# The last chunk's forward and backward scans interleaved, with the long convolution dealt out between their steps

## The chip, the cores and the metric

One core of one Trainium2 chip runs the whole kernel in one launch. The metric is the device time of an execution in microseconds (us); lower is better. The core has five engines with a queue of instructions each: TensorE (PE, matrix products and transposes), VectorE (DVE), ScalarE (ACT), GpSimd (POOL) and SyncE (SP), which here only issues DMA transfers. Each engine works its queue strictly in order and waits on semaphores for the others. Matrix products write to PSUM, of which this kernel uses eight banks of 128 x 512 f32; everything else lives in SBUF or in device memory.

## What is computed

One layer of a generator over 2048 tokens of width 1024, with 256 context tokens ahead. One projection feeds three mixers, whose outputs are concatenated, projected, scaled and added to the input; a layer norm and a gated MLP with a 3x3 depthwise convolution follow.

```python
def _mixer(h, lp, h0_f, h0_b):
    proj = h @ lp['w_in']
    a_val, a_gate, _, _, _, u_pool = jnp.split(proj, IN_SPLITS, axis=-1)
    ya = _conformer_conv(a_val, a_gate, lp)
    yb, st_f, st_b = _ssd_branch(proj, lp, h0_f, h0_b)
    yc = _pool_mixer(u_pool, lp)
    return jnp.concatenate([ya, yb, yc], axis=-1) @ lp['w_out'], st_f, st_b

def _conformer_conv(a_val, a_gate, lp):          # 256 channels, 31 taps, 15 tokens to either side
    u = a_val * jax.nn.sigmoid(a_gate)
    u = _dwconv1d(u, lp['conv_dw_w'], lp['conv_dw_b'], (CONV_K // 2, CONV_K // 2))
    u = jax.nn.silu(_layer_norm(u, lp['conv_ln_g'], lp['conv_ln_b']))
    return u @ lp['conv_pw_w'] + lp['conv_pw_b']

def _gated_rms_norm(y, z, gain):                 # y = forward scan + backward scan
    v = y.astype(F32) * jax.nn.silu(z.astype(F32))
    v = v * lax.rsqrt(jnp.mean(v * v, axis=-1, keepdims=True) + RMS_EPS)
    return (v * gain.astype(F32)).astype(z.dtype)
```

The SSD branch is a linear recurrence over tokens (8 heads of 64, state of 128, a 4-tap convolution ahead), run once forward and once backward. A scan is cut into sub-chunks: within one, a masked product of tokens with tokens; between them, a state of 128 x 512 is handed on. The forward scan goes up the tokens, the backward scan down, so the backward scan of the last sub-chunk needs no other one.

## The kernel before

Tokens are worked in four chunks of 512, a scan in sub-chunks of 128 (four a chunk; `f3_2` is the forward scan of chunk 3, sub-chunk 2, `b3_2` the backward one). All large products are f32 split into a high and a low part, three matrix products for one (`mm3`, lines L114 to L116; a weight is loaded at L108 and split at L101 and L102).

*Sweep one* takes the chunks upwards (`chunk`). For each it projects the input, applies the 4-tap convolutions of both directions on DVE (L266; forward result `uf` stays in SBUF, backward result `ub` is stored to `scr_ub`), runs the forward scan (its result `y_f` is stored to `scr_yf`, L508), the pool branch (`ps2`, `ps4`, `pr`, `pl`), the 31-tap convolution, and the gate projection z (`zproj`): four products (`zt`, L552), transposed on PE (`zT`, L557), SiLU on ACT (`zs`, L559), stored to `scr_zs` (L560). For chunk 3 z comes last in the code.

The 31-tap convolution (`conv_branch`) is 30 multiply-adds on DVE for each of two halves of 128 channels, 512 tokens each (`c31p`, in a PSUM bank; the bias and tap 0 by ACT, L589). Its result lags by 15 tokens, so chunk 3 has a tail of 15 more columns (`c31t`): 60 multiply-adds of 128x15, at the same line L592. `conv_post` follows: transposes `ct`, copy `ctv`, statistics `cst`, normalization `ctv` (L625), transposes back `cb`, SiLU (L630), product `pw` (L634), result `ya` stored to `scr_yac` (L637). The pool branch stores to `scr_yac` too.

*Sweep two* takes the chunks downwards. `bwd` reloads `ub` as eight tiles of 128x512 (`ubr`, L719, on ACT's queue) and runs the backward scan. `rest` gates each sub-chunk: forward result `yfr` (L732) and `zsr` (L734) are loaded by SP, added and multiplied on DVE (L736, L737), squared on ACT, `rstd` (`rv`, `rr`, `rq`, `yrs`; L121 to L128), scaled (L742), transposed on PE (`yt`, L745) and split (`ybh`, `ybl`). Then `yac` reloads the conv and pool outputs (L702), `mix` projects everything (`o`; its first operand is the conv output), adds it to the input (L782, L783), and the MLP follows after the last chunk. The code of `bwd` for chunk 2 stands ahead of the mix of chunk 3.

A scan step is `ssd_in`, then `ssd_out`. `ssd_in`: load the row of cumulated decays `E` (L353), eight Relu and one Exp on ACT (L355, L356), transposes and token products `bps` on PE, copy `btm` on ACT, mask `gtm` (L367) and `E` times `gtm` on DVE (L369), transposes `xps`, two products `xde`, `xdt` on DVE. `ssd_out`: state product `st` and state update (L406), `yo`, `y` (L414), `yd`, `y` (L419). The banks are few: one for `bps` and `xps` (pool `si`), two for `st`, `yo`, `yd` (`so`), one for all transposes of convolution, pool, z and gate (`lo`), four for the products (`mm`).

What order the instructions take on each engine is set when the program is built: a scheduler takes the code, estimates times, and puts the instructions of all engines in a fixed order, within the dependences and the number of buffers of each tile. It does not follow the order of the code where something else is ready.

## Time and profile before

| what | value |
|---|---|
| runs, us | 2604.77, 2612.76, 2610.20 (median 2610.2) |
| the profiled execution, us | 2605.01 |
| its span, us | 2603.3 |
| its mean granted PE clock | 0.957 |
| PE, DVE, ACT, POOL busy, share of the span | 92%, 69%, 44%, 50% |

The span runs from the first to the last instruction. A granted clock of 1 is full speed of TensorE. The profile gives the time by line and operation, the idle time of each engine with what ended it ("DVE x <- ACT y" is idle time of DVE in front of x, which y released), and the chain of work that ended last. The stretch in which sweep one ends and sweep two starts lies at about 553 to 871 us of the span. Below, `DVE`, `PE` and so on stand ahead of a line number; a name ends in `_f` or `_b` by the direction of the scan.

### The profile page before, as it was taken

Reading aid. Unit: us, or ns where it says so; the run is one execution under the profiler, and the core shown is the slowest. Engines: PE = TensorE matmul, PEld = TensorE weight load, DVE = VectorE, ACT = ScalarE, POOL = GpSimd, SP = SyncE. Lnnn points to the kernel's source line nnn. Section 1 sums busy time; section 2 is a strip of 40 time slices with the busy share of each in tenths; the row PEclk is TensorE's granted clock in tenths of the full one; section 3 lists DMA queues with packets and bytes.
Section 4 is the critical chain, followed back from the end, with each engine's and each line's share of the span. In section 5 each row is a group of like instructions: output and inputs, shape, how many; then the busy total and the mean of one; then the engine's idle time right before and its main releaser. Section 6 shows DMA issues by size and latency. Waiting matters only on the chain.

```text
span 2603.3 us, 31634 instructions
## 1 busy us (share of the span) xinstructions
PE 2403.8 (92%) x11338; PEld 1987.1 (76%) x11338; DVE 1791.9 (69%) x2681; ACT 1149.7 (44%) x1765; POOL 1303.9 (50%) x928
## 2 busy tenths in 40 slices
PE   6998999998768978899999999999999999899996
PEld 3776877776647767789998878888878888788885
DVE  5767968698948586576556596665696664876645
ACT  2657566747354334343334333344333344233342
...
GB/s 277 255 141 145 129 139 111 138 108 119 135 112 200 206 186 193 175 210 90 90 90 134 97 146 100 97 124 105 122 128 99 97 117 96 151 97 106 97 98 73
DMA packets 125838, 347.01 MB, mean 133 GB/s; under 512 B 19680, under 2 KB 24176, under 8 KB 125680
## 3 DMA queue, kind: packets, MB, share of 16 engines
...
## 4 chain that ended last, share of the span: by engine, by line
PE 61%; DVE 20%; DMA 6%; ACT 6%; issue 3%; POOL 2%; SPq 0%; ACTq 0%; DVEq 0%; POOLq 0%
PE d L114 6%; PE d L116 6%; PE d L115 6%; PE ug L114 5%; PE ug L115 5%; PE ug L116 5%; PE uv L114 5%; PE uv L115 5%; PE uv L116 5%; DVE c31p L592 2%; DVE fa L886 1%; DVE xt L783 1%; ACT E_f L355 1%; DMA x_c<-in_xT 1%; PE o L114 1%
## 5 line engine op out<-in xcount | busy, mean ns | idle before, releaser
L886 DVE SCALAR_TENSOR_TENSOR fa<-gbuf,cols,fa 128x512 f32<-128x512 f32 x704 | 523.6, 753 | 225.0 <-ACT fa L882 202.7
L916 DVE TENSOR_TENSOR gl<-g,gh 128x512 fp32r<-128x512 f32 x176 | 195.6, 1122 | 218.3 <-ACT gh L915 196.9
L102 POOL TENSOR_TENSOR wl_d<-wr_d,wh_d 128x1024 fp32r<-128x1024 f32 x88 | 222.1, 2524 | 210.7 <-ACT wh_d L101 210.7
L114 PE MATMUL ug<-h2h,wh_ug 128*128 128x512 f32 (+3 forms) x880 | 309.9, 352 | 18.1 <-DVE g L894 10.7
L102 POOL TENSOR_TENSOR wl_uv<-wr_uv,wh_uv 128x1024 fp32r<-128x1024 f32 x88 | 220.3, 2504 | 207.9 <-ACT wh_uv L101 207.9
L102 POOL TENSOR_TENSOR wl_ug<-wr_ug,wh_ug 128x1024 fp32r<-128x1024 f32 x88 | 214.5, 2437 | 192.1 <-ACT wh_ug L101 192.1
L115 PE MATMUL ug<-h2l,wh_ug 128*128 128x512 f32 (+3 forms) x880 | 309.0, 351 | 0.0
L116 PE MATMUL ug<-h2h,wl_ug 128*128 128x512 f32 (+3 forms) x880 | 308.7, 351 | 0.0
L114 PE MATMUL uv<-h2h,wh_uv 128*128 128x512 f32 x704 | 275.3, 391 | 9.0 <-DVE g L894 8.8
L115 PE MATMUL uv<-h2l,wh_uv 128*128 128x512 f32 x704 | 274.9, 390 | 0.0
L116 PE MATMUL uv<-h2h,wl_uv 128*128 128x512 f32 x704 | 274.6, 390 | 0.0
L115 PE MATMUL d<-wl_d,gh 128*128 128x512 f32 x704 | 273.9, 389 | 0.0
L114 PE MATMUL d<-wh_d,gh 128*128 128x512 f32 x704 | 273.8, 389 | 0.0
L116 PE MATMUL d<-wh_d,gl 128*128 128x512 f32 x704 | 263.8, 389 | 0.0
L915 ACT ACTIVATE gh<-g 128x512 fp32r<-128x512 f32 x176 | 110.9, 630 | 247.5 <-PE d L115 225.8
L114 PEld LDWEIGHTS ug<-h2h,wh_ug 128*128 128x128 f32 x880 | 168.8, 192 | 38.5 <-DVE g L894 11.9
L101 ACT ACTIVATE wh_ug<-wr_ug 128x1024 fp32r<-128x1024 f32 x88 | 93.2, 1059 | 221.4 <-PE uv L115 189.1
L115 PEld LDWEIGHTS ug<-h2l,wh_ug 128*128 128x128 f32 x880 | 168.8, 192 | 17.7
L116 PEld LDWEIGHTS ug<-h2h,wl_ug 128*128 128x128 f32 x880 | 168.6, 192 | 16.8
L592 DVE SCALAR_TENSOR_TENSOR c31p<-gl,cols,c31p 128x512 f32<-128x512 f32 x232 | 162.2, 746 | 20.3 <-ACT c31p L589 20.0
L114 PEld LDWEIGHTS uv<-h2h,wh_uv 128*128 128x128 f32 x704 | 132.6, 188 | 36.5 <-DVE g L894 9.6
L101 ACT ACTIVATE wh_uv<-wr_uv 128x1024 fp32r<-128x1024 f32 x88 | 93.2, 1059 | 144.7 <-PE ug L115 95.6
(391 smaller groups left out, 5485.6 us busy)
## 6 DMA issues: line engine op xcount, KB each, us to landing
wr_ug<-in_w_up SPq DMA_DIRECT2D x88, 512.0 KB, 3.6
wr_uv<-in_w_up SPq DMA_DIRECT2D x88, 512.0 KB, 3.5
wr_d<-in_w_dn SPq DMA_DIRECT2D x88, 512.0 KB, 3.6
wm<-in_w_mod SPq DMA_DIRECT2D x64, 256.0 KB, 3.8
wr_x<-in_w_x SPq DMA_DIRECT2D x32, 512.0 KB, 3.7
wr_o<-in_w_o SPq DMA_DIRECT2D x32, 512.0 KB, 4.1
wm<-in_w_mod SPq DMA_DIRECT2D x16, 512.0 KB, 8.0
x_c<-in_xT SPq DMA_DIRECT2D x32, 256.0 KB, 3.8
```

What stands on the lines that cost most here:

```text
L101: nc.scalar.activation(hi, src, AF.Copy)
L102: nc.gpsimd.tensor_tensor(lo, src, hi.bitcast(F32), AL.subtract)
L114: nc.tensor.matmul(out, a[0], b[0], start=first, stop=False)
L115: nc.tensor.matmul(out, a[0], b[1], start=False, stop=False)
L116: nc.tensor.matmul(out, a[1], b[0], start=False, stop=last)
L355: nc.scalar.activation(E[:, h, :], E[:, h, :], AF.Relu, bias=cum[:, d, s, h : h + 1], scale=-1.0)
L592: nc.vector.scalar_tensor_tensor(to[:, :m], gl[:, j, o + k : o + k + m], w[k], acc[:, :m], AL.mult, AL.add)
L783: nc.vector.scalar_tensor_tensor(xs[i][:, hsl], xs[i][:, hsl], ALPHA, m, AL.mult, AL.add)
L886: nc.vector.scalar_tensor_tensor(acc, G[:, dr : dr + 8, dc : dc + GW], wc[i], acc, AL.mult, AL.add)
L915: nc.scalar.activation(gh, gt[k], AF.Copy)
L916: nc.vector.tensor_tensor(gl, gt[k], gh.bitcast(F32), AL.subtract)
```

## The change

Chunk 3's forward and backward scan are put into one function, `turn`, which takes the place of the end of `chunk(3)` and of `bwd(3)`. It writes the steps in the order f0, f1, b3, b2, f2, b1, f3, b0, each with the start of the next one ahead of it.

- The backward inputs come in 128-token pieces (`ubs`, four loads of 512 KB on ACT's queue, two buffers) in place of the eight `ubr`.
- In the backward steps, `E` is in two tiles of 128x512, and `E`, `xde`, `xdt` and `xD` lie in buffers of the projection's input (`hhi`, `hlo`) that are no longer in use.
- A sub-chunk is gated when the later of its two directions is done: forward 0, 1 and backward 3, 2 are stored to `scr_yf` and read back by the gate; forward 2, 3 and backward 1, 0 are not stored.
- z is split in `zpart` and `zturn`; its projections stand in the code between the first forward steps and its transposes after the start of backward step 3. The pool branch stands between the two halves of the z projections.
- The 15-column tail becomes, for each channel half, one product of 128x465 (15 columns by 31 taps, the input read through overlapping windows, `slide`) and one sum over the taps (`tensor_reduce`); its `conv_post` comes first.
- The main convolution is a generator that hands back after every ten taps and is resumed between the steps, first half of the channels, then the second; its `conv_post` runs when it is used up, between the gates of sub-chunks 1 and 3.

Cut to its core, the diff:

```diff
+def slide(v, m, taps):
+    return bass.AP(tensor=v.tensor, offset=v.offset, ap=[list(v.ap[0]), [1, m], [1, taps]])
...
+        def buf(tag, alt):
+            if spare:
+                return self.p1.tile([P, 512], F32R, tag=alt, name=f"{tag}_{name}", bufs=8).bitcast(F32)
+            return sp.tile([P, 512], F32, tag=tag, name=f"{tag}_{name}", bufs=SB)
+
         r = {}
         if want_y:
-            E = sp.tile([P, 8, P], F32, tag="E", name=f"E_{name}", bufs=SB)
-            nc.sync.dma_start(E, self.s[f"arow{key}"][d, s].unsqueeze(0).to_broadcast([P, 8, P]))
+            if spare:
+                E = [buf(f"E{g}", "hhi").rearrange("p (h l) -> p h l", h=4) for g in range(2)]
+            else:
+                E = [sp.tile([P, 8, P], F32, tag="E", name=f"E_{name}", bufs=SB)]
+            m = 8 // len(E)
+            Eh = [E[h // m][:, h % m, :] for h in range(8)]
+            for i, e in enumerate(E):
+                nc.sync.dma_start(e, self.s[f"arow{key}"][d, s, i * m : (i + 1) * m].unsqueeze(0).to_broadcast([P, m, P]))
...
-            E4 = E.rearrange("p (g h) l -> p g h l", g=2)
-            nc.vector.tensor_tensor(E4, E4, gtm.unsqueeze(2).to_broadcast([P, 2, 4, P]), AL.mult)
-            r["E"] = E
+            n = 2 // len(E)
+            for i, e in enumerate(E):
+                E4 = e.rearrange("p (g h) l -> p g h l", g=n)
+                nc.vector.tensor_tensor(E4, E4, gtm[:, i * n : (i + 1) * n, :].unsqueeze(2).to_broadcast([P, n, 4, P]), AL.mult)
+            r["E"] = Eh
...
-        xde = sp.tile([P, 512], F32, tag="xde", name=f"xde_{name}", bufs=SB)
+        xde = buf("xde", "hlo")
...
+        if last:
+            return hs, fwd, out
         self.ppool(c, hs)
         for s in range(SB - 1):
             fwd(s)
-        if not last:
-            self.zproj(c, hs)
+        self.zproj(c, hs)
         for s in range(NSUB):
             out(s)
             if s + SB - 1 < NSUB:
                 fwd(s + SB - 1)
         self.pool_branch(c)
-        self.conv_branch(c)
-        if last:
-            self.zproj(c, hs)
+        for _ in self.conv_branch(c):
+            pass
+
+    def turn(self, hs, fwd, out):
+        c = NCH - 1
+        nc, sp, pa = self.nc, self.sp, self.pa
+        cat = [None] * 8
+        ybh = pa.tile([P, 4, 512], F32R, tag="ybh", name=f"ybh{c}", bufs=1)
+        ybl = pa.tile([P, 4, 512], F32R, tag="ybl", name=f"ybl{c}", bufs=1)
+        ub, ins = {}, {}
+
+        def load(s):
+            b = pa.tile([P, 8, P], F32, tag="ubs", name=f"ubs{c}_{s}", bufs=2)
+            t0 = c * CH + s * P
+            nc.scalar.dma_start(b, self.s["ub"][:, :, t0 : t0 + P].rearrange("j p t -> p j t"))
+            ub[s] = [b[:, j, :] for j in range(8)]
+
+        def first(s):
+            ins[s] = self.ssd_in(1, c, s, ub[s], 0, True, f"b{c}_{s}", spare=True)
+
+        def scan(s):
+            return self.ssd_out(1, c, s, ins[s], f"b{c}_{s}")
+
+        rows = self.s[f"yf{c}"]
+        conv = self.conv_branch(c)
+        load(3)
+        load(2)
+        self.ppool(c, hs)
+        fwd(0)
+        next(conv, None)
+        zt = self.zpart(c, hs, 0, 2)
+        self.pool_branch(c)
+        out(0)
+        fwd(1)
+        next(conv, None)
+        zt = zt + self.zpart(c, hs, 2, 4)
+        first(3)
+        self.zturn(c, zt)
+        next(conv, None)
+        first(2)
+        y = scan(3)
+        nc.sync.dma_start(rows[3 * P : 4 * P, :], y)
+        load(1)
+        next(conv, None)
+        out(1)
+        fwd(2)
+        next(conv, None)
+        y = scan(2)
+        nc.sync.dma_start(rows[2 * P : 3 * P, :], y)
+        load(0)
+        first(1)
+        next(conv, None)
+        y = out(2, False)
+        fwd(3)
+        self.gate(c, 2, y, ybh, ybl)
+        next(conv, None)
+        y = scan(1)
+        first(0)
+        self.gate(c, 1, y, ybh, ybl)
+        for _ in conv:
+            pass
+        y = out(3, False)
+        self.gate(c, 3, y, ybh, ybl)
+        y = scan(0)
+        self.gate(c, 0, y, ybh, ybl)
+        for i in range(4):
+            cat[2 + i] = (ybh[:, i, :], ybl[:, i, :])
+        return cat
 
...
         n = self.width(c)
-        accs, tails = [], []
+        wv = self.cols[:, COFF["dw_w"] : COFF["dw_w"] + 2 * TAPS].rearrange("p (j k) -> p j k", k=TAPS)
+        if n > CH:
+            m = n - CH
+            tail = self.lp.tile([P, 2, 16], F32, tag="c31t", name=f"c31t_{c}", bufs=1)
+            for j in range(2):
+                prod = self.lp.tile([P, CH], F32, tag="c31", name=f"c31q_{c}_{j}", bufs=4)[:, 0 : m * TAPS].rearrange("p (t k) -> p t k", k=TAPS)
+                g = gl[:, j, CH : CH + m + TAPS - 1]
+                nc.vector.tensor_tensor(prod, slide(g, m, TAPS), wv[:, j, :].unsqueeze(1).to_broadcast([P, m, TAPS]), AL.mult)
+                nc.vector.tensor_reduce(tail[:, j, 0:m], prod, mybir.AxisListType.X, AL.add)
+                nc.scalar.activation(tail[:, j, 0:m], tail[:, j, 0:m], AF.Identity, bias=self.col("dw_b", j))
+            self.conv_post(c, [tail[:, j, 0:m] for j in range(2)], m, CH)
+        accs = []
         for j in range(2):
-            w = [self.col("dw_w", j * TAPS + k) for k in range(TAPS)]
             out = self.lp.tile([P, CH], F32, tag="c31", name=f"c31_{c}_{j}", bufs=4)
-            parts = [(out, self.bank(self.mm, f"c31p_{c}_{j}"), 0, CH)]
-            if n > CH:
-                tail = self.lp.tile([P, 16], F32, tag="c31t", name=f"c31t_{c}_{j}")
-                parts.append((tail, tail, CH, n - CH))
-                tails.append(tail[:, 0 : n - CH])
-            for dst, acc, o, m in parts:
-                nc.scalar.activation(acc[:, :m], gl[:, j, o : o + m], AF.Identity, bias=self.col("dw_b", j), scale=w[0])
-                for k in range(1, TAPS):
-                    to = dst if k == TAPS - 1 else acc
-                    nc.vector.scalar_tensor_tensor(to[:, :m], gl[:, j, o + k : o + k + m], w[k], acc[:, :m], AL.mult, AL.add)
+            acc = self.bank(self.mm, f"c31p_{c}_{j}")
+            nc.scalar.activation(acc, gl[:, j, 0:CH], AF.Identity, bias=self.col("dw_b", j), scale=wv[:, j, 0:1])
+            for k in range(1, TAPS):
+                nc.vector.scalar_tensor_tensor(out if k == TAPS - 1 else acc, gl[:, j, k : k + CH], wv[:, j, k : k + 1], acc, AL.mult, AL.add)
+                if k % 10 == 0:
+                    yield
             accs.append(out)
         self.conv_post(c, accs, CH, 0)
-        if n > CH:
-            self.conv_post(c, tails, n - CH, CH)
 
...
+            self.gate(c, s, self.ssd_out(1, c, s, ins[s], f"b{c}_{s}"), ybh, ybl)
```

The order of the built programs at the places that matter. Names carry the chunk, the sub-chunk and a running number. First DVE, where chunk 2's convolution has ended and chunk 3's 4-tap convolutions (`ca_f`, `ca_b`, `ub`, `uf`) run; before:

```order
L592 SCALAR_TENSOR_TENSOR c31t_3_1_5935<-gl3_5002,cols_105,c31t_3_1_5935 128x15
L266 SCALAR_TENSOR_TENSOR ca_b3_2_5483<-raw3_2_5471,cols_105,ca_b3_2_5483 128x515
L266 SCALAR_TENSOR_TENSOR uf3_2_5475<-raw3_2_5471,cols_105,ca_f3_2_5476 128x512
L592 SCALAR_TENSOR_TENSOR c31t_3_1_5935<-gl3_5002,cols_105,c31t_3_1_5935 128x15
L266 SCALAR_TENSOR_TENSOR ub3_2_5482<-raw3_2_5471,cols_105,ca_b3_2_5483 128x515
L592 SCALAR_TENSOR_TENSOR c31t_3_1_5935<-gl3_5002,cols_105,c31t_3_1_5935 128x15 x2
L592 SCALAR_TENSOR_TENSOR c31p_3_0_5869<-gl3_5002,cols_105,c31p_3_0_5869 128x512 x4
```

After, the tail stands right behind the last tap of chunk 2 (`c31_2_1`):

```order
L691 SCALAR_TENSOR_TENSOR c31_2_0_4739<-gl2_3724,cols_105,c31p_2_0_4740 128x512
L691 SCALAR_TENSOR_TENSOR c31_2_1_4772<-gl2_3724,cols_105,c31p_2_1_4773 128x512
L681 TENSOR_TENSOR c31q_3_0_5650<-gl3_5002,cols_105 128x465
L681 TENSOR_TENSOR c31q_3_1_5654<-gl3_5002,cols_105 128x465
L424 TENSOR_TENSOR state_f2_3_4693<-state_f2_3_4693,st_f2_3_4690 128x512
L682 TENSOR_REDUCE c31t_3_5649<-c31q_3_0_5650 128x15
L682 TENSOR_REDUCE c31t_3_5649<-c31q_3_1_5654 128x15
L432 TENSOR_TENSOR y_f2_3_4699<-yo_f2_3_4696,ex_c2_3714 128x512
```

The tail has gone from 60 rows among the 4-tap convolutions to four rows ahead of them. DVE again, around the last tap of chunk 3's convolution (`c31_3_1`, out of `c31p_3_1`); before:

```order
L406 TENSOR_TENSOR state_b3_3_6329<-state_b3_3_6329,st_b3_3_6326 128x512
L592 SCALAR_TENSOR_TENSOR c31p_3_1_5934<-gl3_5002,cols_105,c31p_3_1_5934 128x512
L592 SCALAR_TENSOR_TENSOR c31_3_1_5933<-gl3_5002,cols_105,c31p_3_1_5934 128x512
L414 TENSOR_TENSOR y_b3_3_6335<-yo_b3_3_6332,ex_c3_4992 128x512
L367 TENSOR_TENSOR gtm_b3_2_6388<-bps_b3_2_6381,tri_121 128x256
L369 TENSOR_TENSOR E_b3_2_6370<-E_b3_2_6370,gtm_b3_2_6388 128x1024
L419 TENSOR_TENSOR y_b3_3_6335<-y_b3_3_6335,yd_b3_3_6338 128x512
L375 TENSOR_TENSOR xde_b3_2_6396<-xps_b3_2_6391,ex_c3_4992 128x512
```

After, where the next product of statistics, `cst3_0_0_0`, is row 930, and the normalization ends with row 964:

```order
L691 SCALAR_TENSOR_TENSOR c31p_3_1_6089<-gl3_5002,cols_105,c31p_3_1_6089 128x512 x2
L432 TENSOR_TENSOR y_f3_2_6248<-yo_f3_2_6245,ex_c3_4992 128x512
L691 SCALAR_TENSOR_TENSOR c31p_3_1_6089<-gl3_5002,cols_105,c31p_3_1_6089 128x512
L383 TENSOR_TENSOR gtm_b3_1_6213<-bps_b3_1_6206,tri_121 128x256
L691 SCALAR_TENSOR_TENSOR c31_3_1_6088<-gl3_5002,cols_105,c31p_3_1_6089 128x512
L387 TENSOR_TENSOR E0_b3_1_6192<-E0_b3_1_6192,gtm_b3_1_6213 128x512
L387 TENSOR_TENSOR E1_b3_1_6193<-E1_b3_1_6193,gtm_b3_1_6213 128x512
L437 TENSOR_TENSOR y_f3_2_6248<-y_f3_2_6248,yd_f3_2_6251 128x512
```

The last tap stood within the first backward step (`b3_3`), behind all four forward steps; it stands now at the start of the third backward step (`b3_1`), with the last forward step (`f3_3`) still behind it. PE ahead of the first `o` product of chunk 3's mix; before, from the tail's `pw` on:

```order
L634 MATMUL pw3_512_1_6095<-c31t_3_0_5870,pw_274 128x15
L634 MATMUL pw3_512_1_6095<-c31t_3_1_5935,pw_274 128x15
...
L557 MATMUL zT3_3_6257<-ident_107,zt3_0_6132 128x128
L557 MATMUL zT3_3_6257<-ident_107,zt3_1_6165 128x128
L557 MATMUL zT3_3_6257<-ident_107,zt3_2_6198 128x128
L557 MATMUL zT3_3_6257<-ident_107,zt3_3_6231 128x128
L400 MATMUL st_b2_3_6699<-xde_b2_3_6688,btm_b2_3_6678 128x256 x2
L114 MATMUL o3_0_0_7022<-wh_o3_0_0_7027,yah3_0_6622 128x512
L115 MATMUL o3_0_0_7022<-wl_o3_0_0_7028,yah3_0_6622 128x512
```

After:

```order
L733 MATMUL pw3_0_1_6379<-c31_3_0_5696,pw_274 128x512
L733 MATMUL pw3_0_1_6379<-c31_3_1_6088,pw_274 128x512
L391 MATMUL xps_b2_0_6879<-ident_107,ubr2_0_6605 128x128
L391 MATMUL xps_b2_0_6879<-ident_107,ubr2_1_6607 128x128
L391 MATMUL xps_b2_0_6879<-ident_107,ubr2_2_6609 128x128
L391 MATMUL xps_b2_0_6879<-ident_107,ubr2_3_6611 128x128
L827 MATMUL yt3_1_6463<-ident_107,yfr3_1_6444 128x128 x4
L827 MATMUL yt3_3_6511<-ident_107,yfr3_3_6492 128x128 x4
L118 MATMUL o3_0_0_6975<-wh_o3_0_0_6980,yah3_0_6575 128x512
L119 MATMUL o3_0_0_6975<-wl_o3_0_0_6981,yah3_0_6575 128x512
```

z's transposes (`zT`) have moved away, some 110 rows up among the backward steps 3 and 2; the main part's `pw` and the gates' `yt3_1` and `yt3_3` stand here now, and the last, `yt3_0`, follows twelve `o` products later, at row 2525. SP's transfers at the same place; before:

```order
L560 DMA scr_zs3_79<-zs3_0_6238 128x512
L560 DMA scr_zs3_79<-zs3_1_6246 128x512
L560 DMA scr_zs3_79<-zs3_2_6254 128x512
L560 DMA scr_zs3_79<-zs3_3_6262 128x512
L734 DMA zsr3_3_6324<-scr_zs3_79 128x512
L732 DMA yfr3_2_6403<-scr_yf3_78 128x512
L683 DMA g1r_6618<-scr_g1_58 128x1024
L702 DMA yac3_0_6620<-scr_yac3_80 128x512
L702 DMA yac3_1_6626<-scr_yac3_80 128x512
```

After:

```order
L368 DMA E_b2_1_6777<-scr_arow2_77 128x1024
L368 DMA E_b2_0_6858<-scr_arow2_77 128x1024
L736 DMA scr_yac3_80<-ya3_0_0_6376 128x512
L368 DMA E_b1_3_7397<-scr_arow1_71 128x1024
L782 DMA g1r_6571<-scr_g1_58 128x1024
L801 DMA yac3_0_6573<-scr_yac3_80 128x512
L736 DMA scr_yac3_80<-ya3_0_1_6382 128x512
L817 DMA zsr3_0_6542<-scr_zs3_79 128x512
L869 DMA xt3_0_6967<-in_x 128x1024
```

The stores of `zs` and the first `zsr` stood ahead of the reload `yac3_0` and have moved up (the stores to rows 320 to 323); now the stores of the conv output `ya` stand around it, and the last gate's `zsr3_0` behind the second of them.

More of the change, by code (lines that the diff above doesn't have):

```diff
@@ L70, in run @@
             self.shift(self.p1, 64)
-            self.sweep1()
+            turn = self.sweep1()
             e5.close()
@@ L74, in run @@
             self.ngr = self.row(self.pa, t["norm_row"], "ngr")
-            top = self.bwd(NCH - 1)
+            top = self.turn(*turn)
             self.shift(self.pa, 96)
@@ L337, in dt_path, with ssd_in @@
         return rows
-    def ssd_in(self, d, key, s, ui, off, want_y, name):
+    def ssd_in(self, d, key, s, ui, off, want_y, name, spare=None):
         nc, sp = self.nc, self.sp
@@ L417, in ssd_out @@
         for h in range(8):
-            nc.tensor.matmul(yd[:, h * 64 : (h + 1) * 64], r["E"][:, h, :], r["xdt"][:, h * 64 : (h + 1) * 64], start=True, stop=True)
+            nc.tensor.matmul(yd[:, h * 64 : (h + 1) * 64], r["E"][h], r["xdt"][:, h * 64 : (h + 1) * 64], start=True, stop=True)
         nc.vector.tensor_tensor(y, y, yd, AL.add)
@@ L461, in sweep1 @@
         for c in range(NCH):
-            self.chunk(c)
+            res = self.chunk(c)
             if c == 0:
                 self.mod_finish()
+        return res
     def chunk(self, c):
@@ L504, in fwd, with out @@
             ins[s] = self.ssd_in(0, c, s, uf, s * P, True, nm)
-        def out(s):
+        def out(s, keep=True):
             y = self.ssd_out(0, c, s, ins[s], f"f{c}_{s}")
-            nc.sync.dma_start(self.s[f"yf{c}"][s * P : (s + 1) * P, :], y)
+            if keep:
+                nc.sync.dma_start(self.s[f"yf{c}"][s * P : (s + 1) * P, :], y)
+            return y
         ins = {}
+        if last:
+            return hs, fwd, out
         self.ppool(c, hs)
@@ L547, in zproj, with zpart @@
         nc, t, p1, n = self.nc, self.t, self.p1, CH
+        self.zturn(c, self.zpart(c, hs, 0, 4))
+    def zpart(self, c, hs, j0, j1):
+        nc, t, p1, n = self.nc, self.t, self.p1, CH
         zt = []
-        for j in range(4):
+        for j in range(j0, j1):
             pz = self.proj(self.load_w(t["w_x"][14 + j], f"z{c}_{j}"), hs, n, f"z{c}_{j}")
@@ L553, in zproj, with zturn @@
             zt.append(z)
+        return zt
+    def zturn(self, c, zt):
+        nc, p1 = self.nc, self.p1
         for i in range(4):
@@ L709, in yac, with gate @@
         return cat
+    def gate(self, c, s, y, ybh, ybl):
+        nc, p2 = self.nc, self.pa
+        nm = f"{c}_{s}"
+        rs_ = slice(s * P, (s + 1) * P)
+        yf = p2.tile([P, 512], F32, tag="yf", name=f"yfr{nm}", bufs=YB)
+        nc.sync.dma_start(yf, self.s[f"yf{c}"][rs_, :])
+        zs = p2.tile([P, 512], F32, tag="yf", name=f"zsr{nm}", bufs=YB)
+        nc.sync.dma_start(zs, self.s[f"zs{c}"][rs_, :])
+        nc.vector.tensor_tensor(yf, yf, y, AL.add)
+        nc.vector.tensor_tensor(yf, yf, zs, AL.mult)
+        sq = p2.tile([P, 1], F32, tag="sq", name=f"sq{nm}")
+        nc.scalar.activation(zs, yf, AF.Square, accum_out=sq)
+        rs = p2.tile([P, 1], F32, tag="yrs", name=f"yrs{nm}")
+        self.rstd(rs, sq, p2, 1, f"y{nm}", scale=1.0 / DSSM, eps=RMS_EPS)
+        nc.vector.scalar_tensor_tensor(yf, yf, rs, self.ngr, AL.mult, AL.mult)
+        tp = self.bank(self.lo, f"yt{nm}")
+        for i in range(4):
+            nc.tensor.transpose(tp[:, i * P : (i + 1) * P], yf[:, i * P : (i + 1) * P], self.ident)
+        tp3 = tp.rearrange("p (i l) -> p i l", i=4)
+        nc.scalar.activation(ybh[:, :, rs_], tp3, AF.Copy)
+        nc.vector.tensor_tensor(ybl[:, :, rs_], tp3, ybh[:, :, rs_].bitcast(F32), AL.subtract)
     def bwd(self, c):
```

30 lines of the change are left out of this document (5 added, 25 removed).

## The prediction

> **What bounds the kernel now.** The page's span first, then its group rows of the engines over the whole program:
>
> ```profile
> span 2603.3 us, 31634 instructions
> PE 2403.8 (92%) x11338; PEld 1987.1 (76%) x11338; DVE 1791.9 (69%) x2681; ACT 1149.7 (44%) x1765; POOL 1303.9 (50%) x928
> ```
>
> TensorE (PE) carries the program as a whole, but the change touches one stretch of it, from the end of chunk 2's convolution to the end of chunk 3's mix. That stretch I found by the times of the lines that change, and cut it at four places: the start of the main convolution of chunk 3 (641.8), its end inside the scans (713.6), the first `o` matmul of the mix (785.9), the last of the mix (871.1). The columns are length, busy time of PE, of its weight loads, of VectorE (DVE), ScalarE (ACT), GpSimd (POOL), granted PE clock, DMA share, GB/s:
>
> ```profile
> 552.80:641.80 89.00, 77.60 (x361) 61.67 (x359) 81.53 (x173) 51.16 (x83) 36.50 (x29) 0.96 0.32 101
> 641.80:713.60 71.80, 55.17 (x242) 44.06 (x243) 69.83 (x99) 33.59 (x62) 35.77 (x23) 0.80 0.43 136
> 713.60:785.90 72.30, 43.53 (x206) 32.62 (x204) 38.41 (x75) 34.37 (x77) 19.54 (x16) 0.71 0.39 129
> 785.90:871.10 85.20, 76.49 (x363) 62.81 (x364) 73.17 (x107) 37.62 (x79) 49.28 (x34) 0.93 0.59 183
> 552.80:871.10 318.30, 252.79 (x1170) 201.16 (x1169) 262.94 (x452) 156.73 (x299) 141.09 (x102) 0.86 0.43 137
> ```
>
> Stages one and two are DVE's: 81.5 of 89.0 and 69.8 of 71.8 us busy. Stage three, the backward scan alone, has no bound: PE 43.5 and DVE 38.4 of 72.3. Stage four is PE's, 76.5 of 85.2. The waits of DVE and of PE in that stretch (us in total, times, longest), and the chain that ended last at 773 to 786 (start, us):
>
> ```profile
> DVE yfr L737 <- DMA zsr<-scr_zs: 20.1, 3, 16.2
> DVE gtm_b L367 <- ACT btm_b L364: 9.6, 3, 7.1
> DVE c31p L592 <- ACT c31p L589: 7.4, 1, 7.4
> PE cb L629 <- DVE ctv L625: 8.4, 2, 6.7
> ...
> 773.25 1.13 PE zT L557 x4
> 775.08 1.98 DMA scr_zs<-zs
> 778.39 6.81 DMA yac<-scr_yac
> 785.90 0.79 PE o L114
> ```
>
> So stage three ends like this: z of chunk 3 is transposed last, goes to memory and comes back, and the SyncE queue (SP) reaches the reload of the conv output only after that. DVE stands 16.2 us for `zsr`.
>
> **The change, part by part.** Its own time of this execution is 2605.0 us (1.7 round the span); the median of the three runs shown is 2610.2, 5.2 above. I make the sum against the 2605.0.
>
> *1. The 15-column tail.*
>
> ```profile
> L592 DVE SCALAR_TENSOR_TENSOR c31t<-gl,cols,c31t 128x15 f32<-128x15 f32 x60 | 25.8, 438 | 3.1 <-ACT c31t L589 3.1
> L592 DVE SCALAR_TENSOR_TENSOR c31t<-gl,cols,c31t x60: 193/222/2223, 552.8 to 634.1; 128x15 f32<-128x15 f32 x60
> L736 DVE TENSOR_TENSOR yfr<-yfr,y_b 128x512 f32<-128x512 f32 x8 | 5.5, 684 | 0.7 <-DMA yfr<-scr_yf 0.7
> L737 DVE TENSOR_TENSOR yfr<-yfr,zsr 128x512 f32<-128x512 f32 x8 | 9.2, 1152 | 20.1 <-DMA zsr<-scr_zs 20.1
> L800 DVE BATCH_NORM_STATS2 st_l<-xt 128x6 f32<-128x512 f32 x7 | 4.8, 680 | 0.0
> ```
>
> All sixty lie in stage one; out go 25.8 us of DVE. In come two products of 465 columns and two sums over 31 taps. No row shows a tensor reduce, nor the product's overlapping read; the nearest is the statistics instruction, which also folds many columns into few, 680 ns for 512, and the plain products, 684 to 1152 ns for 512. Scaled by 465/512: four instructions at 0.62 to 1.05 us, 2.5 to 4.2 in all; I take 3. The Trainium skill, VectorE: DVE Perf Modes, section Rules for kernel authors, speaks against this part: it calls the tensor reduce the slowest DVE operation and advises to restructure. At its one-times rate, which fp32 products have too in its table, the sum would stay at 3 by my estimate; no run here shows it yet.
>
> DVE saves about 23 there, but stage one cannot shrink so far: PE is busy 77.6 of its 89.0. I count what PE waited for DVE (6.7 of the 8.4) and some of the small gaps, 9 us. Ends: nothing, if ScalarE's order sets the end of the stage (DVE's 7.4 wait at its end is for ScalarE), and 11.4, all PE idle. By the order shown with the change, the tail no longer stands between the short convolutions on DVE; its sixty rows of before are the ones that `ctv`, and so PE's `cb`, queued behind.
>
> *2. Both scans side by side, the convolution dealt out.*
>
> ```profile
> L592 DVE SCALAR_TENSOR_TENSOR c31p<-gl,cols,c31p 128x512 f32<-128x512 f32 x74 | 52.8, 746 | 7.6 <-ACT c31p L589 7.4
> L369 DVE TENSOR_TENSOR E_b<-E_b,gtm_b 128x1024 f32<-128x1024 f32 x8 | 9.9, 1236 | 0.1
> L400 PE MATMUL st_b<-xde_b,btm_b x20: 379/632/795, 716.0 to 783.6; 128*128 128x256 f32 x20
> ...
> 743.40 2.06 PE st_b L400 x4
> ```
>
> Four backward steps alone began 716.0 to 743.4, 9.1 us apart, of which DVE works some 5 (E, the mask at 0.4 and five operations at 0.68). The DVE work of stages two to four stays: the same eight scan steps, gates and 60 main taps, with each mask product E in two halves (128x1024 at 1236 ns becomes two of 128x512, by L736 684 each: 0.13 more in each of four steps). Its floor is 69.8+38.4+73.2 = 181.4 of 229.3 us; 47.9 are idle. What fills: the taps that DVE did in stage two now stand between the steps of both scans, so `gtm_b`, which waits for ScalarE (9.6), has something ahead of it. And z is transposed before the second backward step, four stores to memory long before their readers, so the 20.1 for `zsr` goes. I count both, 29.7. Ends: 0, as in part 3 both can come back elsewhere, and 36, where DVE would be at 94% and PE, at 175.2 of 193, at 91%.
>
> *3. What is late next.* The convolution ended ahead of the backward scan; now its last tap is DVE row 888, its normalization ends 76 rows later, and its output is the mix's first operand. On PE, where z's transposes stood ahead of the first `o`, `pw` and two gates' `yt` stand now, with the third `yt` twelve `o` matmuls on; the backward steps of chunk 2, between the `o` matmuls before, come ahead of nearly all of them. On SP `zsr3_0` has moved behind both conv stores and, in a ring of three buffers, behind a `yt`. The prices, of transfers (KB, us to landing), of instructions (ns), and of places in the chain (start, us):
>
> ```profile
> scr_yac<-ya SPq DMA_DIRECT2D x2, 256.0 KB, 2.0
> yac<-scr_yac SPq DMA_DIRECT2D x6, 248.5 KB, 3.2
> zsr<-scr_zs SPq DMA_DIRECT2D x9, 256.0 KB, 3.1
> ubr<-scr_ub ACTq DMA_DIRECT2D x22, 256.0 KB, 4.9
> E_b<-scr_arow SPq DMA_DIRECT2D x10, 512.0 KB, 4.0
> ...
> L630 ACT ACT_TABLE_LOAD  x2: 1283/1283/1283, 739.3 to 760.2; - x2
> L630 ACT ACTIVATE c<-cb,cols x2: 777/777/777, 740.6 to 742.1; 128x512 f32<-128x512 f32 x2
> L634 PE MATMUL pw<-c,pw x8: 592/592/595, 746.9 to 752.4; 128*128 128x512 f32 x8
> ...
> 842.21 1.38 DVE yfr L737
> 853.48 1.09 PE yt L745 x4
> ...
> 785.90 0.79 PE L114 MATMUL o<-wh_o,yah 128*128 128x512 f32 x1 [1.69 <-ACT yah L101]
> 789.05 0.63 PE L115 MATMUL o<-wl_o,yah 128*128 128x512 f32 x1
> ```
>
> From the normalized conv to the first `o`: a table load 1.3, two activations 1.6, the `pw` products 2.4, a store 2.0, a load 3.2, with the splits some 12 us. Ahead of it on PE stand two and a half backward steps of chunk 2. I take 7 as exposed; ends 0 and 12. Then the third `yt`: 3.1 for `zsr3_0`, and a gate, 11.3 us in the one shown from its product to its transpose, some 8 with DVE less loaded; against it the first twelve `o` matmuls, eight of which took 3.2 us at the cold clock, so 4.8. Left 6 to 10; I take 7, low end 0.
>
> *4. The pieces `ubs`.* Four loads of 512 KB in 512-byte rows for eight of 256 KB in 2-KB rows. No row shows such rows: from 4.0 us (E_b, 512 KB) to 4 x 4.9 = 19.6, if each row costs what a long one does; I take 9.8, twice `ubr`, the row it is nearest to. Each new piece waits until the step two before it has read its buffer; a step took 9.1 us when alone, two steps of each direction lie between, so even 19.6 is nearly hidden: 0. The Trainium skill, DMA: Bandwidth & Descriptors, Specifications, puts full rate at 512 bytes and a read-modify-write below: these pieces sit on that bound, so by it too the cost is nothing. On ScalarE's queue the first piece waits for a store of `ub`, 2.0 us by the row of `scr_yac`, with a z weight split behind it; PE has other projections then. 0, up to 2. The stores and reloads dropped (f2, f3, b1, b0 not stored) and added (b3, b2) cancel: 0.
>
> Sum: -9 - 29.7 + 7 + 7 = -24.7, so 2580.3 against 2605.0, and 5.2 more in the runs' median: 2585.
>
> **The rivals.** *Denser still.* PE's clock is part of it:
>
> ```profile
> 760.00:780.00 20.00, 8.21 (x30) 5.79 (x30) 3.69 (x9) 5.11 (x10) 0.00 (x0) 0.50 0.23 81
> 794.00:830.00 36.00, 33.60 (x176) 27.54 (x175) 32.07 (x53) 17.90 (x44) 18.24 (x15) 1.00 0.59 182
> ```
>
> In the empty stretch the clock is at 0.50, in the full one at 1.00. If the fill keeps it up and the two new waits stay hidden: -11.4 - 29.7 = -41, 2569. Against: the steps' chain, PE, ScalarE, DVE and back, remains. The Trainium skill, TensorE: Matmul & The Clock Gate, Part 1, lets the clock drop to half after about 3.4 us of idleness; the trace agrees with 0.50.
>
> *The new waits eat the middle.* The conv output is late by the whole 12 us, the third `yt` by 9.6, and half of the 29.7 returns as waits inside the turn, one PSUM bank serving each step: -9 - 14.9 + 12 + 9.6 = -2, 2608. For it: the stage that was nobody's, three, had 43.5 us of PE and 38.4 of DVE in 72.3. Against: it had nothing to put between, now 60 taps.
>
> *Slower: the late convolution sets the mix.* Of the 363 matmuls of stage four, 192 are the mix's: 192 x 76.5/363 = 40 us, and some 7 until the last row is added. With chunk 2's scan already done, the mix must start by 871 - 47 = 824 to break even, and after 832 it is slower by 0.3%. In my sum it starts at about 799. It takes 33 us more between the last tap and the mix: for instance if the 76 rows up to the normalized conv run at 9 us a step over four steps and more (36), after a turn that has run no faster than stage three did. -24.7 + 36 = +11, 2621.
>
> **How the numbers follow.** My forecast 0.50 (2573 to 2598); denser 0.17; the middle 0.25, from 2598 to 2612, of which half ends 8 us or more below 2610; slower 0.08. About 0.3%, 7.8 us, is what this measurement can tell from no change. Faster: 0.50 + 0.17 + 0.13 = 0.80; same 0.12; slower 0.08. The range runs from 2562, below the denser case, to 2606, inside the middle one; some 0.05 and 0.15 lie outside.
>
> **What would show it.** In the profile after: no 128x15 multiply-add group, two reduces near 0.7 us; stage one's PE gap before `cb` gone; no wait of DVE for `zsr` of 16 us, but a PE wait of `yt` some 5 us after the first `o`; the last tap at about 718 (from 633 on 60 taps at 0.746, six steps at 5 and 10 for the pool and the last short convolutions), the first `o` at about 799, the mix's end at about 846, all from there on as before. Wrong if the last tap comes after 735, if a reduce takes several us, if `gtm_b` waits for `ubs`, or if PE's idle time from tap to mix passes 20 us.

## The result, and the profile after

| | us |
|---|---|
| before, runs beside it | 2604.77 (2599.04 to 2612.76, 7 runs) |
| after | 2595.39 (2586.75 to 2600.78, 7 runs) |
| ratio | 0.9950 [0.9933, 0.9968] |
| after again, beside the second set | 2593.91 against 2608.38, 0.9950 [0.9936, 0.9964] |
| profiled execution, and its span | 2596.35, 2594.6 |

Half a per cent faster: 9 us by the first pair of medians, 14 by the second, where the sum said 25. The page of after opens so:

```profile
span 2594.6 us, 31595 instructions
PE 2405.3 (93%) x11338; PEld 1990.0 (77%) x11338; DVE 1773.0 (68%) x2629; ACT 1153.4 (44%) x1771; POOL 1308.1 (50%) x928
```

DVE does 18.9 us less, PE 1.5 more. To place the gain I count from an instruction that the change leaves alone, the first `gl` product of chunk 3 on DVE (at 547.7 in before, 554.0 in after). The single profiled executions of all kernels reach it between 546.5 and 554.5, ahead of all edits, with the same 2308 PE and 691 DVE instructions behind them, so absolute times mislead by up to 8 us. Three cuts follow it: the end of the last 4-tap convolution, the first `o` of chunk 3's mix, the first `o` of chunk 2's mix. Windows of before, then of after, in the same columns as in the prediction:

```profile
547.70:656.50 108.80, 92.63 (x412) 73.62 (x413) 96.71 (x195) 67.69 (x105) 44.46 (x33) 0.94 0.33 105
656.50:785.90 129.40, 87.78 (x411) 67.90 (x410) 95.09 (x156) 56.49 (x124) 48.12 (x35) 0.76 0.41 131
785.90:865.00 79.10, 70.39 (x336) 57.74 (x337) 67.06 (x97) 36.56 (x78) 46.32 (x33) 0.92 0.61 191
```

```profile
554.00:645.70 91.70, 86.66 (x407) 69.45 (x407) 78.97 (x132) 64.72 (x101) 44.61 (x33) 1.00 0.37 118
645.70:798.30 152.60, 103.56 (x516) 84.27 (x516) 119.17 (x200) 77.10 (x174) 58.80 (x47) 0.81 0.43 138
798.30:857.90 59.60, 54.72 (x237) 44.32 (x238) 36.76 (x64) 21.50 (x39) 34.95 (x23) 0.92 0.61 195
```

The first window lost 17.1 us. The second grew by 23.2 and the third shrank by 19.5: the work was shifted between them (DVE 162.2 to 155.9 in both, PE 158.2 to 158.3), and together they are 3.7 longer (208.5 to 212.2). Behind the third cut the end comes 1.6 sooner (1738.3 to 1736.7). That is -15.0 from the common point on, and the 6.3 by which this execution came late to that point make it -8.7. The repeat's profile gives -19.4, +1.1, -3.8. So in this pair the whole gain stands in the first window, where the new tail is, and none in the two where the scans run side by side.

The new tail, in an answer on its two lines, and the wait that the prediction took out, in the waits of DVE:

```profile
L681 DVE TENSOR_TENSOR c31q<-gl,cols x2: 632/633/634, 573.8 to 574.3; 128x465 f32<-128x465 f32 x2
L682 DVE TENSOR_REDUCE c31t<-c31q x2: 623/624/626, 575.5 to 576.0; 128x15 f32<-128x465 f32 x2
...
DVE yfr L819 <- DMA zsr<-scr_zs: 1.8, 2, 1.4
```

`zsr` costs 1.8 where it cost 20.1, yet the two windows behind the tail are no shorter. What DVE and PE wait for instead, the largest of each (DVE from 645.7 to 798.3, PE to 857.9):

```profile
DVE gtm_b L383 <- ACT btm_b L380: 8.5, 2, 5.8
DVE ybl L830 <- ACT ybh L829: 7.3, 2, 6.9
DVE state_b L424 <- PE st_b L418: 4.9, 4, 2.9
...
PE xps_b L391 <- DVE gtm_b L383: 10.3, 2, 9.5
PE st_b L418 <- DVE xde_b L393: 10.1, 5, 3.0
PE o L118 <- ACT yah L105: 7.4, 2, 7.1
```

Five of the six are links of a scan step or of a gate; `gtm_b` is still there. The sixth is the mix's first operand. Its row on PE, and ScalarE ahead of it:

```profile
798.27 0.79 PE L118 MATMUL o<-wh_o,yah 128*128 128x512 f32 x1 [7.05 <-ACT yah L105]
...
794.40 0.33 ACTq L840 DMA_DIRECT2D ubr<-scr_ub  x1
794.77 2.15 ACT L370 ACTIVATE E_b<-E_b,cum_c 128x128 f32<-128x128 f32 x7 [4.19 <-DMA ubr<-scr_ub]
796.83 0.58 ACT L829 ACTIVATE ybh<-yt 128x512 fp32r<-128x512 f32 x1
797.31 0.39 ACT L370 ACTIVATE E_b<-E_b,cum_c 128x128 f32<-128x128 f32 x1
797.60 0.62 ACT L105 ACTIVATE yah<-yac 128x512 fp32r<-128x512 f32 x1
```

ScalarE stood 4.19 us at the issue of a load of chunk 1's `ubr` and then worked Relus of a chunk 1 step, while `yah`, on which the whole mix waited, was queued behind both.

### The profile page after: what moved, and what is told of

It reads as the page before. It is cut to its first block, busy times and chain, and to the rows that moved or that the text cites. A ratio compares the mean times of both kernels' runs of the same rounds, so it can differ in the third digit from the quotient of the medians.

```text
span 2594.6 us, 31595 instructions
## 1 busy us (share of the span) xinstructions
PE 2405.3 (93%) x11338; PEld 1990.0 (77%) x11338; DVE 1773.0 (68%) x2629; ACT 1153.4 (44%) x1771; POOL 1308.1 (50%) x928
## 4 chain that ended last, share of the span: by engine, by line
PE 65%; DVE 18%; ACT 6%; DMA 5%; issue 4%; POOL 2%; SPq 0%; ACTq 0%; DVEq 0%; POOLq 0%
PE d L118 6%; PE d L120 6%; PE d L119 6%; PE ug L118 5%; PE uv L118 5%; PE uv L119 5%; PE ug L119 5%; PE uv L120 5%; PE ug L120 5%; DVE fa L987 1%; PE o L118 1%; DVE c31p L691 1%; PE o L119 1%; PE o L120 1%; DMA wm<-in_w_mod 1%
## 5 line engine op out<-in xcount | busy, mean ns | idle before, releaser
L118 PEld LDWEIGHTS ug<-h2h,wh_ug 128*128 128x128 f32 x880 | 168.4, 191 | 38.4 <-DVE g L995 16.0
```

The source lines that it names most:

```text
L118: nc.tensor.matmul(out, a[0], b[0], start=first, stop=False)
```

## The experiments

Times against before on the same chip. The windows are those above, each from one profiled execution; "sum" is the difference to before from the common point to the end.

| kernel | to last 4-tap | to first `o` | to chunk 2's mix | to the end | sum | median, difference | ratio [95%] |
|---|---|---|---|---|---|---|---|
| before | 108.8 | 129.4 | 79.1 | 1738.3 | | | |
| after | 91.7 | 152.6 | 59.6 | 1736.7 | -15.0 | -9.4 | 0.9950 [0.9933, 0.9968] |
| after again | 89.4 | 151.6 | 58.0 | 1734.5 | -22.1 | -14.5 | 0.9950 [0.9936, 0.9964] |
| tail alone | 92.4 | 129.8 | 75.5 | 1741.2 | -16.7 | -16.0 | 0.9940 [0.9925, 0.9956] |
| turn, old tail | 109.1 | 132.0 | 59.3 | 1742.9 | -12.3 | -18.8 | 0.9929 [0.9916, 0.9942] |
| z early | 102.9 | 144.2 | 70.5 | 1737.8 | -0.2 | -3.1 | 0.9986 [0.9972, 1.0001] |
| after, `ubr` on GpSimd | 91.5 | 141.9 | 61.1 | 1737.4 | -23.7 | -24.5 | 0.9910 [0.9896, 0.9924] |
| tail alone, `ubr` on GpSimd | 92.2 | 131.4 | 79.4 | 1740.8 | -11.8 | -11.9 | 0.9963 [0.9950, 0.9976] |
| no taps | 89.7 | 127.5 | 67.0 | 1737.3 | -34.1 | -33.9 | 0.9883 [0.9865, 0.9902] |
| taps by 15 | 91.7 | 133.4 | 71.0 | 1738.3 | -21.2 | -21.5 | 0.9927 [0.9914, 0.9941] |
| own banks | 91.7 | 148.2 | 62.2 | 1737.5 | -16.0 | -13.5 | 0.9950 [0.9931, 0.9969] |
| own banks, by 15 | 91.6 | 135.6 | 71.5 | 1739.5 | -17.4 | -13.3 | 0.9950 [0.9932, 0.9968] |
| all banks | 91.7 | 145.0 | 62.5 | 1737.6 | -18.8 | -14.0 | 0.9950 [0.9932, 0.9969] |

Sum and median agree to 0.1 to 8 us, so a difference of under 8 us between two profiles decides nothing by itself. Added up from the common point, chunk 2's mix starts after 317.3 us before, 297.7 with the tail alone, 300.4 with the turn alone, 303.9 with both, and 294.5 with both and `ubr` on GpSimd.

**After again.** The unchanged kernel beside the second set.

> The changed kernel again, on the same chip as the three beside it, so that they can be set against it. 9 to 16 us under before.

The ratio repeats to the fourth digit.

**The tail alone.** Before, with only the new tail:

```diff
+            for j in range(2):
+                ...
+                nc.vector.tensor_tensor(prod, slide(g, m, TAPS), ...)
+                nc.vector.tensor_reduce(tail[:, j, 0:m], prod, ...)
-                parts.append((tail, tail, CH, n - CH))
```

> The kernel before, with nothing changed but the 15-column tail of chunk 3 (two products and two sums in place of 60 multiply-adds, its post-processing first). Theory A (the tail is nearly the whole gain, the turn gives nothing net): chunk 3's last 4-tap convolution ends 8 to 11 us earlier, the first o matmul of its mix comes about as much earlier, the median is 6 to 10 us under before. Theory B (the tail is hidden behind ScalarE and PE in stage one and the turn makes the gain): the last 4-tap convolution ends 0 to 3 us earlier and the median stays within 3 us of before.

Measured 0.9940: the tail by itself is worth as much as the whole change. Its windows:

```profile
546.50:638.90 92.40, 84.90 (x388) 68.02 (x389) 79.68 (x134) 65.46 (x102) 44.49 (x33) 0.97 0.37 117
638.90:768.70 129.80, 92.06 (x435) 71.31 (x434) 100.55 (x159) 63.39 (x132) 47.13 (x36) 0.79 0.41 133
```

The gain lies in the first, and it is larger than theory A allowed: 16.4 us in the window, 16.0 in the median. The second is as long as before.

**The turn with the old tail.** After, with the sixty multiply-adds back:

```diff
-                nc.vector.tensor_tensor(prod, slide(g, m, TAPS), ...)
-                nc.vector.tensor_reduce(tail[:, j, 0:m], prod, ...)
+                for k in range(1, TAPS):
+                    nc.vector.scalar_tensor_tensor(tail[:, 0:m], ...)
```

> The changed kernel with the old tail: 60 multiply-adds of 128x15 again, everything else as changed (interleaved scans, early z, dealt-out convolution). Theory A: within 3 us of before, or up to 4 slower, since the first o matmul comes at least as late as in the changed kernel and the stage one gain is gone. Theory B: 6 to 10 us under before, as the changed kernel itself.

Measured 0.9929. So the turn by itself is worth 18.8 us, and both theories fall: the one that leaves it nothing, and the one that gives it 6 to 10. Its first window is as long as before's; the other two, with the scans and the mix:

```profile
656.20:788.20 132.00, 99.22 (x509) 79.09 (x507) 111.13 (x190) 71.79 (x159) 53.07 (x45) 0.82 0.46 144
788.20:847.50 59.30, 52.93 (x244) 43.57 (x242) 44.71 (x69) 25.80 (x51) 35.56 (x24) 0.94 0.67 218
```

Together they are 17.2 shorter than before's, all of it by the last. The window ahead of the first `o` holds 509 matmuls in place of 411, so more of chunk 2's scan is done by then, and chunk 3's mix takes 59.3 in place of 79.1. What the two edits do not do is add: 0.60% and 0.71% alone, 0.50% together. The first `o` of this kernel has no wait for `yah`; a later one waits 3.3.

**z early.** Before, with z's projection ahead of the scan steps in chunk 3 also, so that the wait for `zsr` goes while the scans stay as they are:

```diff
-        if not last:
-            self.zproj(c, hs)
+        self.zproj(c, hs)
...
-        if last:
-            self.zproj(c, hs)
```

> The kernel before, with z of chunk 3 projected and transposed where the other chunks do it (ahead of the scan steps) and nothing else. My sum took the 20 us wait for zsr as lost time. If it is: no DVE wait over 3 us for zsr, the first o matmul 8 to 12 us earlier, the median 6 to 12 us under before. If something else stands right behind it (the tail's pw, the reload of the conv output): first o within 4 us of before and the median within 3 us.

Measured 0.9986 with an interval that holds 1. No wait for the load of `zsr` is left among DVE's waits from 550 to 875; the longest of them now:

```profile
DVE ybl L746 <- ACT ybh L745: 12.0, 3, 7.9
DVE ca_f L266 <- ACT ca_f L263: 11.2, 1, 11.2
DVE gtm_b L367 <- ACT btm_b L364: 9.4, 5, 5.1
```

The largest wait of the stretch can go, and the time stays. The first `o` came 8.9 us later from the common point, which neither expectation held. The edit does more than take the wait out: z's products and transposes now stand ahead of the scan steps, and other waits appear. So the 20.1 were not time to be had by this edit; whether they were slack or were paid for again elsewhere, the run does not tell.

**`ubr` on GpSimd's queue.** After, with one line changed, so that ScalarE no longer issues these loads:

```diff
-            nc.scalar.dma_start(b, self.s["ub"][j, :, cs])
+            nc.gpsimd.dma_start(b, self.s["ub"][j, :, cs])
```

> The changed kernel with the reloads ubr of chunks 2, 1 and 0 issued by GpSimd in place of ScalarE. In the changed kernel PE waits 7.1 us for yah ahead of the first o, and ScalarE stands behind an ubr issue that waits 4.2 us for an earlier transfer, with chunk 1's Relus next. Theory A: with the issue away from ScalarE the wait falls under 2 us, the first o comes 4 to 8 us earlier and the median is 3 to 7 us under the changed kernel (12 to 16 under before). Rival: the reload yac itself or the gates are as late, so the first o moves by less than 2 us and the median by less than 2; or GpSimd's own work is held up and the time is 3 us or more above the changed kernel.

Measured 0.9910, its interval clear of after's. ScalarE ahead of the first `o` at 782.16, which PE now starts without a wait:

```profile
780.07 0.57 ACT L398 ACTIVATE xD_b<-xps_b 128x512 f32<-128x512 f32 x1
780.55 1.05 ACT L372 ACTIVATE E_b<-E_b 128x1024 f32<-128x1024 f32 x1
781.49 0.62 ACT L105 ACTIVATE yah<-yac 128x512 fp32r<-128x512 f32 x1
...
782.16 0.50 PE L118 MATMUL o<-wh_o,yah 128*128 128x512 f32 x1
```

The first `o` comes 10.9 us sooner from the common point, and 0.4% comes with it, more than theory A gave. This version beats both kernels. Not all of the 10.9 is the wait of 4.19: the second `ya`, the last piece of the conv output, starts 226.7 us after the common point here and 233.8 in after, so 7.1 us are gained ahead of it, where the order built differs too, and 3.8 behind it.

**The same line on the tail alone** tells whether GpSimd's queue is better for these loads in any order.

> The kernel before with the new tail and with ubr issued by GpSimd, without the interleaved scans. Against the changed kernel with ubr by GpSimd (24 us under before) it prices the turn when neither suffers from ScalarE's queue. Theory A (the turn gives nothing net): within 4 us of it, 20 to 27 under before. Theory B (the turn is worth its sum): at most 15 us under before, as the tail alone or less.

Measured 0.9963, no better than the tail alone (0.9940), as theory B has it. So moving these loads pays only in the order that the turn makes. With `ubr` off ScalarE, the turn is worth 0.9910 against 0.9963, some 14 us; with it on ScalarE, 0.9950 against 0.9940, nothing.

**No taps.** This kernel leaves out 58 of the 60 long multiply-adds between the steps, to price them:

```diff
-                nc.vector.scalar_tensor_tensor(...)
+                if c < NCH - 1 or k == TAPS - 1:
+                    nc.vector.scalar_tensor_tensor(...)
```

> The changed kernel without 58 of the 60 multiply-adds of chunk 3's main convolution (its output is left wrong); some 43 us of DVE go, every step, wait and transfer of the two scans stays. Theory C (behind the last 4-tap convolution the interleaved scans are bound by their own chain over PE, ScalarE, DVE and the few banks, not by DVE): the first o matmul comes less than 15 us earlier than in the changed kernel. Theory D (DVE's work bounds the turn): 30 us or more earlier. In between: both.

Measured 0.9883, some 20 us below after; the first `o` comes 27.1 us sooner from the common point, between the two theories. The middle window, and the state products of the first and last backward step of chunk 3:

```profile
641.30:768.80 127.50, 98.16 (x519) 79.97 (x518) 80.33 (x141) 71.54 (x161) 60.87 (x47) 0.85 0.49 160
...
685.21 2.08 PE L418 MATMUL st_b<-xde_b,btm_b 128*128 128x256 f32 x4 [2.39 <-DVE xde_b L393]
731.99 1.13 PE L418 MATMUL st_b<-xde_b,btm_b 128*128 128x256 f32 x4 [2.10 <-DVE xde_b L393]
```

DVE is busy 80 of 127.5 us and the window is as long as before's with all its taps (129.4). Six steps take 7.8 us each here, 10.2 in after: of 43.3 us of taps (58 x 0.746) about half was paid for, half hid. The chain of the steps and DVE's work both bind.

**Taps by 15, banks of their own.** Four more on the version with `ubr` on GpSimd. Fifteen taps between steps instead of ten, so that the convolution ends sooner:

```diff
-                if k % 10 == 0:
+                if k % 15 == 0:
```

> The changed kernel with ubr by GpSimd and the convolution handed back every 15 taps in place of 10, so that its post-processing stands two steps earlier in the code. If the late convolution sets the start of the mix (my rival): the first o 6 to 12 us earlier, 3 to 8 us under the kernel with ubr by GpSimd alone. If the gates set it, or the third yt and the backward steps just move behind the first o: the start of chunk 2's mix within 3 us.

The first `o` came 8.3 us sooner, chunk 2's mix 1.6 later, and the time was no better (0.9927). The late convolution output does hold the first `o`, then, but not the end of the mix. Next, `bps` and `xps` of chunk 3's backward steps in banks of the products, so that the two scans don't share one; then also by 15; then `st`, `yo`, `yd` too:

```diff
-        bps = self.bank(self.si, f"bps_{name}")
+        bps = self.bank(self.mm if spare else self.si, f"bps_{name}")
-        xps = self.bank(self.si, f"xps_{name}")
+        xps = self.bank(self.mm if spare else self.si, f"xps_{name}")
```

> The changed kernel with ubr by GpSimd, and bps and xps of chunk 3's backward steps in banks of the pool mm in place of the one bank of si that both directions share. In the changed kernel the steps follow each other every 9 to 10 us, as the backward steps did alone, and still every 7.4 to 10.6 us without the taps. Theory E (the one si bank makes the steps of the two directions queue): steps of chunk 3 every 5 to 7 us on the mean, the last of them (b0) 10 us or more earlier than in the kernel with ubr by GpSimd, and, as far as the taps and the conv output don't hold the mix instead, 4 to 12 us under it. Theory F (each step's chain over ScalarE and DVE is the limit): gaps of 8.5 us and more as before, time within 3 us of the kernel with ubr by GpSimd.

> The same with the convolution handed back every 15 taps, so that its output comes earlier again. If E holds and the conv output then sets the mix: the first o 5 us or more ahead of the kernel with the separate banks, and up to 6 us under it. If DVE is full from the last 4-tap convolution to the mix by now: within 2 us of it.

> The kernel with ubr by GpSimd and all banks of chunk 3's backward steps (bps, xps and st, yo, yd too) from mm. If the two banks of so queue the steps once si is out of the way: steps every 4 to 6 us and 2 to 6 us under the kernel with bps and xps alone in mm. If not: within 2 us of it, or slower by up to 5, since z and the pool branch want the banks of mm at the same time.

All three 0.9950, worse than the one bank (0.9910). The state product of `b3_0` with banks of its own, and with the shared one:

```profile
734.65 1.85 PE L418 MATMUL st_b<-xde_b,btm_b 128*128 128x256 f32 x4
```

```profile
744.07 1.13 PE L418 MATMUL st_b<-xde_b,btm_b 128*128 128x256 f32 x4 [0.61 <-DVE xde_b L393]
```

From the common points, 550.2 and 548.8, that is 184.4 against 195.3: sharing the one bank costs 10.9 us at the last step. 6.7 of them are there at the first, `b3_3`; the six steps from it to `b3_0` take 9.2 us each against 9.9, so theory E's 5 to 7 did not come. With all banks apart, the first and the last backward step of chunk 3 are:

```profile
682.08 1.60 PE L419 MATMUL st_b<-xde_b,btm_b 128*128 128x256 f32 x4 [0.60 <-DVE gtm_b L383]
719.46 1.13 PE L419 MATMUL st_b<-xde_b,btm_b 128*128 128x256 f32 x4 [0.47 <-DVE xde_b L393]
```

Five steps lie from one to the other here, since `f3_1` comes ahead of `b3_3`, so they take 7.5 us each, and the last one stands 28.2 earlier than with shared banks (167.1 after the common point, 552.4). So the banks do hold the steps. But the taps are then pushed behind them: the last one ends 206.0 after the common point with `bps` and `xps` apart and 213.2 with all, against 173.3, and the first `o` comes later (239.9 and 236.7 against 233.4). That the convolution gives back what the steps gain is not the whole account: with 15 taps between steps as well, the first `o` came 12.7 us sooner than without and the time was the same. What else makes these versions slower stays open.

## Why the prediction was right, and where its sum was wrong

The forecast was faster, 2585 with 2573 to 2598 for its own case; 2595.4 lies at the upper end of that. As a difference it is 9 and 14 us in the two sets of runs, about half of the 25 of the sum. Part 1 gave 8 us more than it was counted for and parts 2 and 3 some 19 less, so that the time came to lie in the range of its own case is partly luck. The sign is not: either edit alone gives it.

*Part 1, -9, measured -17.1* (-16.4 for the tail alone). The four instructions cost 2.5 us, against 3 taken; the reduce at 624 ns stands beside the product's 633. The Trainium skill, VectorE: DVE Perf Modes, Rules for kernel authors, gives the reduce the one-times rate, which agrees; its advice to restructure would not have helped here, where the other form at hand, the sixty small multiply-adds, took 25.8. What was too small was the most that I let this stage give, 11.4, "all PE idle". PE's idle time in the first window fell by 11.1, near that bound, but its busy time is no floor: the same window holds 92.63 us of PE before and 86.66 after, for 412 and 407 matmuls, with a granted clock of 0.94 and 1.00 (92.63 x 0.94 is 87.1). Idle and busy time together make the 17.1. The wait of PE for `ctv` ahead of `cb`, 6.7 here, is gone, as the prediction said.

*Part 2, -29.7, and part 3, +14: together -15.7, measured +3.7 and +1.1.* The step that failed is part 2's: two waits counted as time to be had. For `zsr`, 20.1, the run with z early, which has no such wait, shows about nothing. For `gtm_b`, 9.6, the wait stayed, at 8.5. The second step that failed is the addition: with the old tail the same two windows lost 17.2, near the 15.7 though by a shorter mix, and beside the new tail they lost nothing. And the picture behind part 2, that steps of two scans fill each other's gaps, did not come about. The state products of before from `f3_1` to `b3_0`, and of after from `b3_3` to `b3_0`, six steps each:

```profile
684.25 1.11 PE L400 MATMUL st_f<-xde_f,btm_f 128*128 128x256 f32 x4
743.40 2.06 PE L400 MATMUL st_b<-xde_b,btm_b 128*128 128x256 f32 x4 [1.35 <-DVE xde_b L375]
```

```profile
690.63 2.08 PE L418 MATMUL st_b<-xde_b,btm_b 128*128 128x256 f32 x4 [0.68 <-DVE xde_b L393]
751.69 1.13 PE L418 MATMUL st_b<-xde_b,btm_b 128*128 128x256 f32 x4 [2.82 <-DVE xde_b L393]
```

59.2 and 61.1 us: 9.9 a step one after the other, 10.2 side by side. The taps ran out while work was left. The last one ended at 729.1, and from there to the mix:

```profile
729.10:798.30 69.20, 44.52 (x242) 36.51 (x241) 46.35 (x92) 34.01 (x77) 23.80 (x22) 0.84 0.43 132
```

This is before's stage three again, 72.3 us with PE 43.5 and DVE 38.4, only later. (The prediction ends before's convolution at 713.6; its last tap there starts at 719.5, within the first backward step, and from its end to the first `o` it is 65.7 us with PE 38.9 and DVE 32.0.) PE idles 24.7 in it; "passes 20 us" was named as what would speak against the forecast, and it does. The stage that was nobody's was moved and little better filled.

*Part 3.* The wait for the conv output was there, and its 7.05 on PE against 7 taken is luck, for it did not come by the chain I added up: ScalarE had a DMA issue and another chunk's Relus ahead of `yah`. I had looked at what is queued behind a load on SP and at the first piece `ubs` on ScalarE, not at the loads of the next chunk. The 7 for the third `yt` was nothing: it stands after twelve `o`, without a wait, and the two ahead of the first `o` waited 0.3 and 1.4:

```profile
788.49 0.66 PE L827 MATMUL yt<-ident,yfr 128*128 128x128 f32 x4 [0.34 <-ACT ya L735]
790.56 0.66 PE L827 MATMUL yt<-ident,yfr 128*128 128x128 f32 x4 [1.41 <-DVE ybl L830]
803.55 0.86 PE L827 MATMUL yt<-ident,yfr 128*128 128x128 f32 x4
```

The mix was mis-sized too, though it is no term of the sum and only sets the point from which the change would be slower: 47 us from its first `o` to its end, by equal shares of 363 matmuls; it took 65.1 (798.3 to 863.4). The mean held many small matmuls: in before's own profile the `o` matmuls take some 53 us of PE, not 40. And 45 others still stand between the mix's 192 up to the third cut. The first `o` at 798.3 against 799 is no success, since 799 was worked back from that 47, and counted from the common point it came at 244.3, where 799 would have been 251.3.

*Part 4, 0, held.* The pieces on ScalarE's queue, with the time to landing:

```profile
L557 ACTq DMA_DIRECT2D ubs<-scr_ub x4: 366/378/534, 648.7 to 715.1; - x4
...
DMA to landing us min/median/max: 3.8/4.0/7.9
```

512 KB in 512-byte rows landed in 4.0 at the median and 7.9 at most, like `E_b` with 4.0; of my two ends the low one was right. The Trainium skill, DMA: Bandwidth & Descriptors, Specifications, puts full rate at 512 bytes; these rows were no slower than long ones, which agrees.

*The rivals.* The middle one, 2598 to 2612, is nearest by mechanism: half of part 2's gain and more came back, and the largest waits left are links inside the turn. Its banks are part of it (28.2 us at the last step when none is shared), but giving the steps their own was no remedy. The late convolution holds the first `o`, by the run with 15 taps, but not the mix's end, so its price of 36 did not come; the denser case is out, by the 10.2 us a step. One correction of words: by the code the convolution's `conv_post` runs when the seventh resumption finds it used up, behind the gate of sub-chunk 2, not between those of 1 and 3.

*Open.* Without the wait on ScalarE's queue, tail and turn together give 0.90%, less than 0.60 and 0.71 added. In after, the 4-tap convolutions end 17.4 us sooner than in the turn with the old tail, yet the first `o` comes 3.2 later. The run with `ubr` on GpSimd gives back 10.9 of that; some 10 are still lost. The traces show where: of the 17.6 that this run is ahead of the turn with the old tail at the end of the 4-tap convolutions, 11.4 are left at `b3_3` (136.0 against 147.4 from the common point), 6.9 at `b3_0` and 7.7 at the first `o`. So they go in the steps, ahead of `b3_3` and in the six after it, 9.9 us each against 9.1. That both edits fill the same slack would fit; it is argued, not shown.
